# Column sums of the later modulation on TensorE: eight one-column products, or four products with 32 columns of ones and two transposes

## The chip, the cores and the metric

The kernel runs on one core of one Trainium2 chip. Its time is the device time of that core in microseconds (us). A core has TensorE (matrix products, PE in the profile; PEld is its weight load), VectorE (DVE), ScalarE (ACT), GpSimd (POOL) and SyncE (SP), which issues the transfers (DMA). Each engine works through its own instructions in a fixed order; semaphores make one wait for another. Products are written to PSUM, everything else lies in SBUF.

## What is computed

One layer of a streaming encoder, for 512 prompt frames and 64 sample frames, in float32. A condition vector c of each of the two streams gives six modulation vectors of 2048; two of them shift and scale the input, the others gate the residuals and shift and scale the input of the second part.

```python
mod = jax.nn.silu(c) @ w_ada[l] + b_ada[l]
sh1, sc1, g1, sh2, sc2, g2 = jnp.split(mod[:, None, :], N_MOD, axis=-1)
h = rmsnorm(x, norm1[l]) * (1 + sc1) + sh1
mix, s_a, s_b, s_c = token_mixers(h, ...)
x = x + g1 * mix
h = rmsnorm(x, norm2[l]) * (1 + sc2) + sh2
f, s_f = conv_ffn(h, ...)
x = x + g2 * f
y = rmsnorm(x, final_norm)
```

`token_mixers` is an input projection, two kinds of recurrence (GLA with 4 heads, gated DeltaNet with 8) and an output projection; `conv_ffn` is an up projection, a short convolution and a down projection. `w_ada` is 2048 x 12288 numbers, 100.7 MB.

## The kernel before

Feature vectors lie on the 128 partitions, frames along the free dimension. Every float32 weight tile is split into two parts, wh (ScalarE) and wl (VectorE, line 600), and each group of a projection is six products of 288 columns (lines 512 and 514).

The stages in order of time: a head, in which the modulation of the first two vectors and the normalised input are made (its `modulation` uses products with 32 output columns, four quarters of PSUM at a time, line 672); the input projection, 50 tiles of 16 groups each (`in_tile`), beside which the recurrences run as jobs; the first half of the output projection, 16 tiles of 8 groups; its second half, 16 tiles, which reads eight further inputs; the up projection; the down projection.

**The later modulation.** Vectors 2 to 5 are made beside the projections. They are 16 blocks of 512 columns of `w_ada` (`ada_blocks(range(8, 24))`). For a block, VectorE multiplies tiles of `w_ada` by the condition and adds them up in two accumulators acc (one for each stream, 128 x 512, lines 770 and 772), a partial sum on each partition; eight loads of 512 KB bring the tiles into the two buffers xr. Line 778 then adds up the 128 partitions: eight products, each with 128 columns of acc as the stationary operand and one column of ones as the moving one. `put_mod` (line 747) adds the bias and stores the result in mod. acc has a single buffer for each stream, so the next block's first multiplication (line 770) waits for the products.

**What sets the order.** `ada_block` is a Python generator: every `yield` is one step. `tick` is called after each projection group and moves it on by `ADA_RATE = 0.65` steps. `rest(n)` yields n times without work. A block has 32 steps with one VectorE operation each and `rest(4)` ahead of the products. Whatever is left of the generator when the first half of the output projection has been issued is then issued in one go (`for _ in K.ada: pass`). A scheduler afterwards places the instructions in each engine's queue.

**Around the end of the blocks.** In the first half of the output projection each tile m takes an xr buffer for the input (`x_tile`, lines 1093 and 1094, transposed on PE), and its result is added to the residual (line 1070, `residual`). The second half's inputs od0 to od7 are loaded by `load_o` (line 1077) into xr and into the three raw buffers in turn, and split by ScalarE (1079) and VectorE (1080). The raw buffers also take the weights (line 598).

Of the kernel before, what the change touches and what calls it, by code (L numbers as in the profile page):

```python
# [8 lines left out]
F32 = mybir.dt.float32  # L9
F32R = mybir.dt.float32r  # L10
I32 = mybir.dt.int32
AF = mybir.ActivationFunctionType
ALU = mybir.AluOpType
# [3 lines left out]
P = 128  # L17
D = 2048
KD = 16
# [76 lines left out]
class Kern:  # L96
# [483 lines left out]
    def raw(self):  # L580
        return self.wp.tile([P, 1024], F32, tag="raw", bufs=3, name=self.name("raw"))
# [161 lines left out]
            nc.sync.dma_start(self.halves(self.early[name, h]), acc[:, :, :HP])  # L743
            nc.sync.dma_start(self.halves(self.sd[name][:, h * TS:(h + 1) * TS]), acc[:, :, HP:])

    def put_mod(self, mi, k0, m):
        self.nc.vector.tensor_tensor(
            self.mod[:, mi, k0:k0 + 4], m,
            self.vec("b_ada", mi * KD + k0, 4).unsqueeze(2).to_broadcast([P, 4, 2]), op=ALU.add)

    def scale_mod(self, out, mi, norm, k0, n=4):

# [4 lines left out]
    def ada_block(self, blk, acc, raw):  # L757

        nc = self.nc
        V, T = nc.vector, nc.tensor  # L760
        acc = [a() for a in acc]
        for k0 in range(0, KD, 2):
            w = raw().rearrange("p (k n) -> p k n", k=2)
            nc.sync.dma_start(w, self.i["w_ada"][0, k0 * P:(k0 + 2) * P, blk * 512:(blk + 1) * 512]
                              .rearrange("(k p) n -> p k n", p=P))
            for k in range(2):
                for s in range(2):
                    col = self.ct[:, s, k0 + k:k0 + k + 1]
                    if k0 + k == 0:
                        V.tensor_scalar_mul(acc[s], w[:, k], col)  # L770
                    else:
                        V.scalar_tensor_tensor(acc[s], w[:, k], col, acc[s], op0=ALU.mult, op1=ALU.add)  # L772
                    yield
        yield from self.rest(4)
        pc = self.bank()
        for j in range(4):
            for s in range(2):
                T.matmul(pc[:, 2 * j + s:2 * j + s + 1], acc[s][:, j * P:(j + 1) * P], self.c["ones"][:, 0:1],  # L778
                         start=True, stop=True)
        self.put_mod(blk // 4, 4 * (blk % 4), pc[:, :8].rearrange("p (j s) -> p j s", s=2))  # L780

    def ada_blocks(self, blocks, acc):
        for blk in blocks:
# [901 lines left out]
```

## Time and profile before

| | |
|---|---|
| median of 3 runs | 2977.57 us (2977.28 to 2982.16) |
| the profiled execution's own time | 2988.47 us |
| its span, first to last instruction | 2986.8 us |
| mean granted TensorE clock | 0.978 |
| PE busy | 2871.2 us, 96% |
| VectorE busy | 2048.5 us, 69% |
| ScalarE busy | 1198.7 us, 40% |
| GpSimd busy | 334.5 us, 11% |
| transfers | 395.55 MB, mean 132 GB/s |
| line 772, multiplications of the blocks | 480 of 754 ns, 341.5 us of VectorE |
| line 778, products of the blocks | 128 products in 256 records |

The busy time of PE is that of its records, whose ends are modelled; how long a group of products holds PE is read from the start of the next. A row of the time line has start, length, engine, line, operation, output and inputs, and a count where rows are merged. The granted clock is 1.00 at full speed. The chain of waits is followed back from the last instruction.

### The profile page before, as it was taken

How to read it: one execution, taken by the hardware profiler on the slowest of the kernel's cores; microseconds unless marked ns; L12 is line 12 of the kernel's file. 1: busy time of each engine (PE TensorE's matmuls, PEld its weight loads, DVE VectorE, ACT ScalarE, POOL GpSimd, SP SyncE). 2: the span in 40 equal slices, each digit the busy share in tenths (PEclk: the TensorE clock that was granted, in tenths of full speed). 3: DMA queues.
4: the chain of work that ended last, by engine and by line, in shares of the span. 5: the costliest groups of instructions: out<-in, count | busy, mean ns of one | idle time of the engine just before them, and what ended most of it. 6: DMA issues, size and time to landing. Idle time of an engine off the chain costs nothing.

```text
span 2986.8 us, 52415 instructions
## 1 busy us (share of the span) xinstructions
PE 2871.2 (96%) x21096; PEld 2774.8 (93%) x21096; DVE 2048.5 (69%) x3198; ACT 1198.7 (40%) x2062; POOL 334.5 (11%) x609
## 2 busy tenths in 40 slices
PE   6998899999899999999999999999999999999998
PEld 3688889999799998999999999999999999999997
DVE  2355776667568867557888888888888865555555
ACT  4235454444435433245444444444444421222223
POOL 0004342232210000000011011111101100000000
PEclk7999999999899999999999999999999999999999
DMA  8964554445454446743333333333333473333221
GB/s 251 286 191 118 143 161 130 129 129 147 123 156 131 140 128 184 201 141 97 111 104 105 113 100 106 113 104 104 114 106 104 133 235 101 111 101 115 86 80 65
DMA packets 535446, 395.55 MB, mean 132 GB/s; under 512 B 59657, under 2 KB 465412, under 8 KB 535204
## 3 DMA queue, kind: packets, MB, share of 16 engines
q1 hardware_dynamic: 535204, 392.21, 44.7%
q8 instruction: 166, 2.72, 0.4%
q14 instruction: 76, 0.62, 0.1%
HBM read 356.47 MB, written 35.67 MB: 131 GB/s over the span
## 4 chain that ended last, share of the span: by engine, by line
PE 80%; DVE 6%; DMA 4%; POOL 4%; ACT 3%; issue 2%; SPq 0%; ACTq 0%; POOLq 0%; DVEq 0%
PE g L512 25%; PE g L514 13%; PE bank L1301 11%; PE bank L1300 11%; PE bank L1302 11%; DVE acc L772 2%; DMA xr<-in_w_ada_dram 1%; PE bank L144 1%; PE bank L672 1%; POOL m L352 1%; POOL m L351 1%; POOL s L138 1%; PE bank L405 1%; PE bank L778 1%; ACT m L1623 1%
## 5 line engine op out<-in xcount | busy, mean ns | idle before, releaser
L1301 PE MATMUL bank<-slot,wh 128*128 128x290 f32 x2464 | 736.2, 299 | 0.0
L1300 PE MATMUL bank<-slot,wh 128*128 128x290 f32 x2464 | 733.9, 298 | 0.0
L1302 PE MATMUL bank<-slot,wl 128*128 128x290 f32 x2464 | 728.0, 295 | 0.0
L512 PE MATMUL g<-slot,wh 128*128 128x288 f32 x3168 | 551.6, 295 | 0.2 <-DVE slot L1070 0.2
L512 PE MATMUL g<-hh,wh 128*128 128x288 f32 x2048 | 470.0, 308 | 2.4 <-ACT wh L599 2.4
L1302 PEld LDWEIGHTS bank<-slot,wl 128*128 128x128 f32 x2464 | 470.6, 191 | 0.0
L1301 PEld LDWEIGHTS bank<-slot,wh 128*128 128x128 f32 x2464 | 469.7, 191 | 0.1
L512 PEld LDWEIGHTS g<-slot,wh 128*128 128x128 f32 x3168 | 465.8, 188 | 0.7 <-DVE slot L1070 0.5
L1300 PEld LDWEIGHTS bank<-slot,wh 128*128 128x128 f32 x2464 | 464.1, 188 | 0.1
L514 PE MATMUL g<-hh,wl 128*128 128x288 f32 x2048 | 461.9, 304 | 1.2 <-DVE wl L600 1.2
L599 ACT ACTIVATE wh<-raw 128x1024 fp32r<-128x1024 f32 x215 | 227.2, 1058 | 586.6 <-PE g L512 571.4
L512 PE MATMUL g<-hl,wh 128*128 128x288 f32 x2048 | 460.6, 304 | 0.0
L1070 DVE SCALAR_TENSOR_TENSOR slot<-g,mod,slot 128x512 f32<-128x512 f32 (+1 forms) x448 | 201.9, 491 | 287.9 <-PE g L514 286.3
L772 DVE SCALAR_TENSOR_TENSOR acc<-xr,ct,acc 128x512 f32<-128x512 f32 x480 | 341.5, 754 | 29.0 <-DMA xr<-in_w_ada_dram 28.1
L512 PEld LDWEIGHTS g<-hh,wh 128*128 128x128 f32 x2048 | 337.7, 193 | 14.7 <-issue 10.2
L514 PEld LDWEIGHTS g<-hh,wl 128*128 128x128 f32 x2048 | 338.9, 193 | 8.3 <-issue 6.0
L514 PE MATMUL g<-slot,wl 128*128 128x288 f32 x1584 | 342.8, 295 | 0.0
L512 PEld LDWEIGHTS g<-hl,wh 128*128 128x128 f32 x2048 | 338.9, 193 | 4.1 <-issue 3.7
L600 DVE TENSOR_TENSOR wl<-raw,wh 128x1024 fp32r<-128x1024 f32 x215 | 262.0, 1219 | 64.9 <-ACT wh L599 63.3
L1247 ACT ACTIVATE wh<-raw 128x1024 fp32r<-128x1024 f32 x176 | 186.0, 1057 | 222.6 <-PE bank L1301 194.2
L514 PEld LDWEIGHTS g<-slot,wl 128*128 128x128 f32 x1584 | 255.3, 188 | 0.0
L1248 DVE TENSOR_TENSOR wl<-raw,wh 128x1024 fp32r<-128x1024 f32 x176 | 215.4, 1224 | 54.0 <-ACT wh L1247 54.0
(346 smaller groups left out, 3180.4 us busy)
## 6 DMA issues: line engine op xcount, KB each, us to landing
raw<-in_w_up_dram SPq DMA_DIRECT2D x176, 512.0 KB
xr<-in_w_ada_dram SPq DMA_DIRECT2D x128, 512.0 KB
raw<-in_w_in_dram SPq DMA_DIRECT2D x100, 512.0 KB
raw<-in_w_down_dram SPq DMA_DIRECT2D x88, 512.0 KB
hraw<-in_w_ada_dram SPq DMA_DIRECT2D x64, 512.0 KB
raw<-in_w_out_dram SPq DMA_DIRECT2D x32, 512.0 KB
slot<-actd SPq DMA_DIRECT2D x44, 288.0 KB
actd<-v SPq DMA_DIRECT2D x44, 256.0 KB
```

The costliest lines, as they stand in the source:

```text
L138: self.nc.gpsimd.tensor_tensor(out[:parts, :n], out[:parts, :n], self.mhalf[:parts, :n], op=ALU.pow)
L512: T.matmul(ps[:, h if bank is None else bank, :n], wh, x[:, h, :n], start=f, stop=False)
L514: T.matmul(ps[:, h if bank is None else bank, :n], wl, ah[:, h, :n], start=False, stop=stop)
L599: nc.scalar.activation(hi[:, :n_], raw[:, :n_], AF.Copy)
L600: nc.vector.tensor_tensor(lo[:, :n_], raw[:, :n_], hi[:, :n_].bitcast(F32), op=ALU.subtract)
L772: V.scalar_tensor_tensor(acc[s], w[:, k], col, acc[s], op0=ALU.mult, op1=ALU.add)
L1070: self.nc.vector.scalar_tensor_tensor(x1[:, :, z], ps[:, :, c], gain[:, q:q + 1], x1[:, :, z], op0=ALU.mult, op1=ALU.add)
L1247: self.nc.scalar.activation(hi, src, AF.Copy)
L1248: self.nc.vector.tensor_tensor(lo, src, hi.bitcast(F32), op=ALU.subtract)
L1300: T.matmul(ps, wh[:, j], hi, start=(c < 3 and j == 0), stop=False, skip_group_check=True)
L1301: T.matmul(ps, wh[:, j], lo, start=False, stop=False, skip_group_check=True)
L1302: T.matmul(ps, wl[:, j], hi, start=False, stop=(j == NPAIR - 1), skip_group_check=True)
```

## The change

In place of the eight products, four are made, with 32 columns of ones as the stationary operand and half of an accumulator (256 columns) as the moving one; each writes 32 partitions of one bank, so that partitions 0 to 31 hold the first half of the first stream's sums 32 times over, and so on. ScalarE copies the bank to SBUF (rows, in one of the three buffers qc of another tile), three steps without work follow, two transposes bring the sums back to the partitions, and `put_mod` is called twice with two tiles of 128 each.

```diff
-    def put_mod(self, mi, k0, m):
+    def put_mod(self, mi, k0, m, n=4):
         self.nc.vector.tensor_tensor(
-            self.mod[:, mi, k0:k0 + 4], m,
-            self.vec("b_ada", mi * KD + k0, 4).unsqueeze(2).to_broadcast([P, 4, 2]), op=ALU.add)
+            self.mod[:, mi, k0:k0 + n], m,
+            self.vec("b_ada", mi * KD + k0, n).unsqueeze(2).to_broadcast([P, n, 2]), op=ALU.add)
...
         yield from self.rest(4)
-        pc = self.bank()
-        for j in range(4):
-            for s in range(2):
-                T.matmul(pc[:, 2 * j + s:2 * j + s + 1], acc[s][:, j * P:(j + 1) * P], self.c["ones"][:, 0:1],
-                         start=True, stop=True)
-        self.put_mod(blk // 4, 4 * (blk % 4), pc[:, :8].rearrange("p (j s) -> p j s", s=2))
+
+        ps = self.bank()
+        for s in range(2):
+            for h in range(2):
+                r = 64 * s + 32 * h
+                T.matmul(ps[r:r + 32, :256], self.c["ones"][:, :32], acc[s][:, h * 256:(h + 1) * 256], start=True, stop=True)
+        rows = self.sp.tile([P, 256], F32, tag="qc", bufs=3, name=self.name("rows"))
+        self.nc.scalar.activation(rows, ps[:, :256], AF.Copy)
+        yield from self.rest(3)
+        pc = self.transpose4(rows.rearrange("p (b t) -> p b t", b=2), 2)
+
+        for h in range(2):
+            self.put_mod(blk // 4, 4 * (blk % 4) + 2 * h, pc.rearrange("p b (s c) -> p b s c", s=2)[:, :, :, 32 * h], 2)
```

With 39 steps instead of 36 a block, and one step's work in another place, the scheduler's order moves on all engines. Lines behind 778 have numbers higher by 7 after the change (1070 becomes 1077, 1077 becomes 1084, 1080 becomes 1087). Two places are shown. The first is PE's queue at the end of the blocks; before, the last block stands ahead of the twelfth tile's transposes in the first half (operands hh and hl):

```order
L512 MATMUL g_13022<-hl_12216,wh_13038 128x288 x2
L514 MATMUL g_13022<-hh_12215,wl_13039 128x288 x2
L778 MATMUL bank_13091<-consts_96,acc_12573 128x1
L778 MATMUL bank_13091<-consts_96,acc_12574 128x1
L778 MATMUL bank_13091<-consts_96,acc_12573 128x1
...
L144 MATMUL bank_13109<-consts_96,xr_13105 128x128 x4
L1099 MATMUL bank_13115<-consts_96,xr_13105 128x64
L512 MATMUL g_13103<-hh_12173,wh_13119 128x288 x2
```

After, on the same engine, it stands behind the last product of the sixteenth tile and ahead of the first of the second half (operands slot):

```order
L512 MATMUL g_13380<-hl_12179,wh_13396 128x288 x2
L514 MATMUL g_13380<-hh_12178,wl_13397 128x288 x2
L780 MATMUL bank_13478<-acc_13201,consts_96 32x256 x2
L780 MATMUL bank_13478<-acc_13202,consts_96 32x256 x2
L144 MATMUL bank_13485<-consts_96,rows_13483 128x128 x2
L512 MATMUL g_13562<-slot_13505,wh_13564 128x288 x2
L512 MATMUL g_13562<-slot_13506,wh_13564 128x288 x2
```

The last block's products have moved from the twelfth tile to the seam between the halves. The second place is VectorE's queue there. Before, behind the last multiplications stand the residuals of the later tiles with the splits of od between them:

```order
L772 SCALAR_TENSOR_TENSOR acc_12574<-xr_12990,ct,acc_12574 128x512
L1070 SCALAR_TENSOR_TENSOR slot_12944<-g_12943,mod,slot_12944 128x2x32
L600 TENSOR_TENSOR wl_13191<-raw_13189,wh_13190 128x1024
L1070 SCALAR_TENSOR_TENSOR slot_13023<-g_13022,mod,slot_13023 128x2x256
L747 TENSOR_TENSOR mod<-bank_13091,cols 128x8
L1070 SCALAR_TENSOR_TENSOR slot_13023<-g_13022,mod,slot_13023 128x2x32
L600 TENSOR_TENSOR wl_13262<-raw_13260,wh_13261 128x1024
L1080 TENSOR_TENSOR slot_13480<-raw_13477,slot_13479 128x576
```

After, from the sixteenth tile's residual on (eight of the ten multiplications left out; raw_13563 is the second half's first weight tile):

```order
L1077 SCALAR_TENSOR_TENSOR slot_13381<-g_13380,mod,slot_13381 128x2x256
L1077 SCALAR_TENSOR_TENSOR slot_13381<-g_13380,mod,slot_13381 128x2x32
L772 SCALAR_TENSOR_TENSOR acc_13201<-xr_13460,ct,acc_13201 128x512
...
L772 SCALAR_TENSOR_TENSOR acc_13202<-xr_13472,ct,acc_13202 128x512
L747 TENSOR_TENSOR mod<-bank_13485,cols 128x4 x2
L1087 TENSOR_TENSOR slot_13506<-xr_13503,slot_13505 128x576
L1087 TENSOR_TENSOR slot_13512<-raw_13509,slot_13511 128x576
L1087 TENSOR_TENSOR slot_13524<-raw_13521,slot_13523 128x576
```

All eight splits of od now stand behind the last block. SyncE's queue has the matching loads in that order too: the last four of `w_ada`, then od0 and od2, later od7, and then the second half's first weights:

```order
L764 DMA xr_13466<-in_w_ada_dram 128x2x512
L764 DMA xr_13472<-in_w_ada_dram 128x2x512
L1084 DMA xr_13503<-od_63 128x576
L1084 DMA xr_13515<-od_65 128x576
L1248 DMA raw_13554<-in_w_up_dram 128x8x128
L1084 DMA xr_13527<-od_67 128x576
L1084 DMA raw_13545<-od_70 128x576
L598 DMA raw_13563<-in_w_out_dram 128x8x128
```

What has moved is the tail of the last block: it stands ahead of the loads that the second half begins with.

## The prediction

> **What bounds the kernel now.** I read the page's busy shares and chain first, then busy time by stage, then the removed line and the last stretch in which it runs. Page:
>
> ```profile
> PE 2871.2 (96%) x21096; PEld 2774.8 (93%) x21096; DVE 2048.5 (69%) x3198; ACT 1198.7 (40%) x2062; POOL 334.5 (11%) x609
> ...
> PE 80%; DVE 6%; DMA 4%; POOL 4%; ACT 3%; issue 2%; SPq 0%; ACTq 0%; POOLq 0%; DVEq 0%
> ```
>
> TensorE (PE) is the bound: 96% busy and 80% of the chain. All sixteen later modulation blocks run between about 200 us and the end of the first half of the output projection. Busy time of that stretch and the next, clock, DMA share and GB/s behind:
>
> ```profile
> 200.00:1297.00 1097.00, 1031.90 (x7562) 989.37 (x7561) 746.31 (x1303) 488.83 (x1111) 211.12 (x433) 0.97 0.52 146
> 1297.00:1399.00 102.00, 102.00 (x775) 102.00 (x774) 70.59 (x127) 55.99 (x102) 4.81 (x17) 1.00 0.34 105
> ```
>
> Here PE stands idle for 65 us of 1097 (6%), and in the second half of the projection for none. What shortens PE's work in the first stretch is therefore worth about 94% of itself; what holds PE up at the end of it is paid in full.
>
> **The removed products.** The line's own view, with who waited for it, and the time line around one block (start, length, count):
>
> ```profile
> L778 PEld LDWEIGHTS bank<-consts,acc x256: 186/192/192, 286.0 to 1259.3; 128*128 128x128 f32 x128
> L778 PE MATMUL bank<-consts,acc x256: 164/250/271, 286.1 to 1259.3; 128*128 128x1 f32 x128
> ...
>   DVE acc L770: 20.6, 9
> ```
> ```profile
> 402.55 0.42 PE L514 MATMUL g<-hh,wl 128*128 128x288 f32 x2
> 402.81 1.84 PE L778 MATMUL bank<-consts,acc 128*128 128x1 f32 x16
> 404.52 0.51 PE L512 MATMUL g<-hh,wh 128*128 128x288 f32 x2
> ```
>
> A block's eight products are 16 records, one weight load each, and hold PE from 402.81 to 404.52: 1.71 us. Sixteen blocks: 27.4 us go.
>
> **The added products.** The same form with 32 output columns stands in the kernel's beginning (line 672, four quarters of PSUM, 512 moving columns), and transposes of four tiles too:
>
> ```profile
> 147.14 0.43 PE L514 MATMUL g<-hh,wl 128*128 128x288 f32 x2
> 147.50 1.07 PE L672 MATMUL bank<-hraw,cs 128*32 128x512 f32 x8
> 148.49 0.54 PE L512 MATMUL g<-hh,wh 128*128 128x288 f32 x2
> ...
> 169.62 0.43 PE L512 MATMUL g<-hl,wh 128*128 128x288 f32 x2
> 169.90 0.60 PE L144 MATMUL bank<-consts,rw 128*128 128x128 f32 x4
> 170.25 0.52 PE L514 MATMUL g<-hh,wl 128*128 128x288 f32 x2
> ```
> ```profile
> 143.06 1.05 PE L672 MATMUL bank<-hraw,cs 128*32 128x512 f32 x2
> ```
>
> One product alone (two records) takes 1.05 us, four take 1.07: they do run together. Two products before 147.50 end their slot at about 147.41, so four products hold PE for 1.08 us up to 148.49. With 256 columns instead of 512 it is between 0.54 (all of it scales) and 1.08 (none does). I take 0.70, nearer to half, because the columns halve and only the change of form stays. Four transposes hold PE from 169.90 to 170.25, so two cost 0.18 (0.35 at most). New price 0.88 us, saving 0.83 us a block, 13.3 us in all (4.5 to 15.8); at 94% **12.5 us**.
>
> Here a rule speaks against the change. The Trainium skill, "TensorEngine Tiling (Array Packing)", section "Key Properties", says that a change of tiling mode drains the engine. The 1.08 us above holds both changes of mode, so the rule can only mean that less of it scales. If none did, the products would cost 0.38 us more a block, 6 us in all, and the sum below would be 2984 us. No run here shows the 256-column form; the rows alone leave both ends open.
>
> **The clock behind the removed products.** Granted clock (third number from the end) behind four of the sixteen groups:
>
> ```profile
> 404.50:408.00 3.50, 3.50 (x28) 3.50 (x28) 3.50 (x8) 3.46 (x6) 0.14 (x1) 1.00 0.13 10
> 728.00:731.40 3.40, 3.40 (x16) 3.40 (x17) 2.18 (x5) 0.00 (x0) 0.00 (x0) 0.50 0.08 6
> 1205.50:1209.00 3.50, 3.50 (x18) 3.50 (x18) 1.92 (x4) 0.00 (x0) 0.00 (x0) 0.55 0.92 280
> 1260.30:1263.70 3.40, 3.40 (x15) 3.40 (x16) 0.80 (x1) 0.52 (x2) 0.00 (x0) 0.53 0.55 143
> ```
>
> After three of the sixteen the clock is at half for about 3.4 us although PE did not wait; the others look like the first row. One-column products evidently can count as rest. Dense 256-column products should not: 3 x 3.4 x 0.48 = **5 us** gained (0 to 5).
>
> **Off PE.** Added are sixteen ScalarE copies and sixteen more VectorE additions. Their nearest rows:
>
> ```profile
> L1052 ACT ACTIVATE m<-bank 128x256 f32<-128x256 f32 x16 | 5.4, 382 | 2.8 <-PE bank L144 2.5
> L747 DVE TENSOR_TENSOR mod<-bank,cols x16: 156/159/168, 289.3 to 1259.6; 128x8 f32<-128x8 f32 x16
> ```
>
> That is 16 x 0.38 = 6.1 us on ScalarE (45% busy in the stretch) and 16 x 0.16 = 2.5 us on VectorE (68%): hidden, 8.6 us at worst. The new wait is PE's transposes on the copy. Behind them all of PE queues, but in the printed order mostly 24 or more projection products (0.13 us each) stand between, over 3 us for a 0.38 us copy: free, except in the first block (six) and the last (none). Against it, VectorE's 20.6 us of waiting for line 778 mostly go, since the new block's first multiplication now comes three steps after the products; and with 39 steps a block instead of 36, fewer multiplications crowd the recurrence's work. Between nothing and 20.6 us; as PE was idle only 6% of the time I take **3 us**.
>
> **What the three extra steps do at the end.** The generator moves 0.65 steps per projection product group. Fifty input tiles of 16 groups and sixteen of 8 make 928 groups, 603 steps. Before, the blocks need 16 x 36 + 1 = 577: they end early. After, they need 16 x 39 + 1 = 625: 22 steps are left when the first half of the projection is over and are issued in one go, and the printed order keeps them there. Before, at this seam, VectorE's last multiplications and PE's first product of the second half:
>
> ```profile
> 1250.80 2.74 DVE L772 SCALAR_TENSOR_TENSOR acc<-xr,ct,acc 128x512 f32<-128x512 f32 x4
> ```
> ```profile
> 1297.18 0.70 PE L512 MATMUL g<-slot,wh 128*128 128x288 f32 x4
> ```
>
> The last multiplications were over 44 us before PE passed to the second half (operand slot instead of hh) without a gap. After, ten multiplications follow the last residual on VectorE, PE's four products stand right behind the last first-half product, and the splits of the second half's inputs and weights behind all of that. Prices:
>
> ```profile
> 1227.87 3.92 DMA xr<-in_w_ada_dram
> ...
> 542.44 5.54 DMA xr<-in_w_ada_dram
> ```
> ```profile
> 2898.59 3.59 DMA raw<-in_w_down_dram
> ...
> 1186.52 6.01 DMA raw<-in_w_out_dram
> ```
> ```profile
> 1297.38 0.94 DVE L1070 SCALAR_TENSOR_TENSOR slot<-g,mod,slot 128x512 f32<-128x512 f32 x2 [2.31 <-PE g L514]
> 1298.24 0.74 DVE L1080 TENSOR_TENSOR slot<-xr,slot 128x576 fp32r<-128x576 f32 x1
> ```
> ```profile
> L599 ACT ACTIVATE wh<-raw 128x1024 fp32r<-128x1024 f32 x215 | 227.2, 1058 | 586.6 <-PE g L512 571.4 <-DMA raw<-in_w_out_dram 10.2 <-PE bank L1301 4.5
> ```
>
> From the end of PE's last first-half product, in us: residual 0.9; two multiplications (2.74 / 4 each) to 2.3, which free the buffer for the last load of w_ada (two xr buffers); that load, between 3.9 and 5.5, say 4.9, to 7.2; its four multiplications to 9.9; products, copy and transposes 1.3, to 11.2; two additions to 11.5; three splits of 0.74, to 13.7, which free the raw buffer of the second half's first weights (SyncE's load waits for the third); that load (3.6 to 6.0), say 5, to 18.7; ScalarE's conversion 1.06, to 19.8. Only then does PE go on. The clock after a shorter pause:
>
> ```profile
> 1164.00:1167.00 3.00, 0.64 (x5) 0.41 (x3) 0.00 (x0) 1.02 (x2) 0.21 (x3) 1.00 0.88 271
> 1167.00:1171.80 4.80, 4.25 (x18) 4.02 (x19) 4.13 (x5) 2.84 (x6) 0.00 (x0) 0.64 0.57 170
> ```
>
> After about 2.4 us without work, 4.8 us ran at 0.64: 1.7 us lost; likewise here, 21.5. Less the 0.9 already charged to the last block: **+21 us**. At least 15 (ten multiplications without a wait, the shortest load, full clock); at most 26 (both longer loads, the clock lost twice).
>
> **Sum.** -12.5 - 5 - 3 + 21 = +0.5 us. The profiled execution (span 2986.8, time 2988.47) would take 2989.0. It lies 0.37% above the median of the runs, 2977.57; taken to the median the forecast is 2978 us, no change. About 0.2%, 6 us, is what a measurement can tell from none, so "within" is 2972 to 2984.
>
> **Rivals.**
> *Slower: the seam is not paid back.* The seam's rows are sure, since nothing stands beside it on PE, while the saving is spread over places where PE next waits for a recurrence anyway, and the clock may dip at other pauses. With 8 us from the products, 3 from the clock, none from VectorE and a seam of 22: +11, 2989 us. It decides once the blocks return under 15 us. For it: 65 us of idle PE beside the blocks. Against it: 94% busy. Chance 0.31.
> *Faster: the recurrence gains.* VectorE's 20.6 us wait stood ahead of work that PE awaits. If 10 us of it show, with 12.5 and 5, and the seam is 17 (loads near 4 us): -10.5, 2967 us. For it: DVE and DMA hold 10% of the chain. Against it: PE idles little. Chance 0.24.
> *The products do not run together.* Four times about 0.55, plus 0.18: 2.4 us a block, +11 instead of -12.5, in all about +24, 3002 us. The equal 1.05 and 1.07 us speak against it. Chance 0.04.
> *Forecast*, 0.41.
>
> **How the numbers follow.** Predicted 2978. The likeliest case's own range is 2972 to 2984. All low bounds together would give 2964 (-15.8 - 5 - 8 + 15), all high ones 2999 (-4.5 + 26); both at once are unlikely. To leave out about 2 in 10 I take 2966 to 2993, which holds the first two rivals' times. Slower 0.31 + 0.04 = 0.35, faster 0.24, same 0.41.
>
> **What would show it.** The new products with a slot near 0.7 us and the two transposes near 0.2; full clock behind every group; VectorE's wait on line 770 nearly gone; PE idle for some 18 us, in two pieces around the last block's products, between the two halves of the output projection; the second half itself unchanged at 102 us. Wrong would be: no gap there (the order would not bind), products above 1.1 us, or a stretch before the seam shortened by far more or less than 20 us.

## The result and the profile after

The changed kernel takes **2994.87 us** (median of 5 runs, 2993.45 to 2998.69) against 2977.57 us (median of 5, 2974.81 to 2984.28): ratio 1.0055, 95% interval 1.004 to 1.007, 17.3 us more. Its profiled execution took 2994.57 us (span 2992.8), so the two profiles lie only 6.0 us of span apart. The first profile of before was simply a long execution: over all runs here the kernel before took between 2968.7 and 2988.3 us, and the profiled one 2988.47. A second execution of it was therefore profiled (e1 below: 2973.54 us, span 2971.8); the second profile, with the first, brackets what is normal.

Busy times and shares of the chain, page of the changed kernel:

```profile
PE 2853.2 (95%) x21000; PEld 2747.7 (92%) x21000; DVE 2047.4 (68%) x3214; ACT 1198.2 (40%) x2076; POOL 340.9 (11%) x609
...
PE 78%; DVE 5%; POOL 5%; DMA 5%; issue 3%; ACT 3%; SPq 1%; ACTq 0%; POOLq 0%; DVEq 0%
```

TensorE is still the bound, busy for 18 us less and with a smaller share of the chain. For the comparison by stage I cut each trace at three instructions that all kernels have (lines in the changed kernel's numbers): ScalarE's first instruction of line 927, just ahead of the blocks; its last copy into an operand slot (line 1107), near the end of the first half of the output projection; and its first instruction of line 1136, in the second half. Windows of before (first profile), of before (second profile) and of after: length, then busy time of PE, PEld, DVE, ACT, POOL, the granted clock, DMA share and GB/s.

```profile
199.40:1291.30 1091.90, 1026.80 (x7524) 984.27 (x7523) 744.27 (x1303) 487.93 (x1108) 211.49 (x435) 0.97 0.52 146
```
```profile
195.30:1277.30 1082.00, 1019.41 (x7525) 976.17 (x7524) 743.88 (x1303) 487.36 (x1109) 216.92 (x435) 0.97 0.52 148
1277.30:1297.70 20.40, 20.40 (x156) 20.40 (x156) 9.44 (x15) 7.58 (x14) 0.19 (x1) 1.00 0.42 123
```
```profile
196.90:1276.00 1079.10, 1007.90 (x7417) 955.64 (x7416) 726.10 (x1294) 483.07 (x1114) 216.95 (x435) 0.97 0.49 141
1276.00:1320.10 44.10, 26.98 (x184) 24.84 (x183) 25.58 (x39) 13.07 (x22) 0.18 (x1) 0.77 0.78 219
1320.10:1407.60 87.50, 87.45 (x662) 87.25 (x662) 65.05 (x117) 50.50 (x96) 5.56 (x16) 1.00 0.34 109
```

The seam grew from 20.4 (20.7 in the first profile) to 44.1 us, with PE busy for 27 of them; the second half itself is as before. The stretch with the blocks became 12.8 us shorter than in the first profile, but only 2.9 us shorter than in the second. It can be split further: the marks of idle time on PE's rows add up to its waits, the granted clock in windows of 1 us adds up to the time lost to it, and PE's busy time less that loss is its work at full clock.

| stretch with the blocks, us | before, first | before, second | after |
|---|---|---|---|
| length | 1091.9 | 1082.0 | 1079.1 |
| PE's work at full clock | 989.3 | 990.4 | 978.9 |
| lost to the clock | 37.5 | 29.0 | 29.0 |
| PE's waits | 64.6 | 62.0 | **70.3** |

Against the second profile the work fell by 11.5 us and the waits rose by 8.3; the clock gave nothing. With 1.6 us ahead of the stretch, 23.7 at the seam and -1.4 behind it, that is the 21.0 us between these two spans.

The new products, view of their line in after (instructions with least, median and greatest duration in ns; below, who waited for them):

```profile
L780 PE MATMUL bank<-acc,consts x128: 379/403/634, 283.1 to 1291.7; 128*32 128x256 f32 x128
...
  ACT rows L782: 40.2, 14
  DVE acc L770: 8.1, 5
```

VectorE's wait for the products (20.6 us before) is mostly gone, as foretold. One block's products on after's time line:

```profile
554.63 0.43 PE L512 MATMUL g<-hl,wh 128*128 128x288 f32 x2
554.90 0.43 PE L514 MATMUL g<-hh,wl 128*128 128x288 f32 x2
555.25 0.64 PE L780 MATMUL bank<-acc,consts 128*32 128x256 f32 x8
555.82 0.53 PE L512 MATMUL g<-hh,wh 128*128 128x288 f32 x2
556.19 0.43 PE L512 MATMUL g<-hl,wh 128*128 128x288 f32 x2
```
```profile
632.55 0.38 PE L144 MATMUL bank<-consts,rows 128*128 128x128 f32 x2
632.68 0.52 PE L512 MATMUL g<-hh,wh 128*128 128x288 f32 x2
633.03 0.43 PE L512 MATMUL g<-hl,wh 128*128 128x288 f32 x2
```

The slot is 0.57 us for the products and 0.13 for the transposes. The neighbours lose a little too: two projection records usually take 0.27 us from start to start, here 0.35 ahead of the products and 0.37 behind them. With that a block costs 0.75 + 0.21 = 0.96 us; the old one, counted alike, 1.79 (slot 1.71, then 0.35). That is 0.83 us a block, the saving that was foretold, though by other terms (below).

PE at the seam, and the clock there:

```profile
1281.84 0.42 PE L514 MATMUL g<-hh,wl 128*128 128x288 f32 x2
1290.65 1.64 PE L780 MATMUL bank<-acc,consts 128*32 128x256 f32 x8 [8.38 <-DVE acc L772]
1292.77 0.69 PE L144 MATMUL bank<-consts,rows 128*128 128x128 f32 x2 [0.48 <-ACT rows L782]
1301.71 1.33 PE L512 MATMUL g<-slot,wh 128*128 128x288 f32 x4 [8.25 <-ACT wh L599]
```
```profile
1293.40:1301.70 8.30, 0.06 (x1) 0.00 (x0) 5.09 (x10) 4.59 (x7) 0.00 (x0) 0.50 0.97 277
1301.70:1306.80 5.10, 5.09 (x25) 4.81 (x26) 3.18 (x3) 1.74 (x2) 0.00 (x0) 0.66 1.10 300
```

From the last first-half product (ends at 1282.26) to the first of the second half: 19.5 us, in two pieces around the last block's products, and 5.1 x 0.34 = 1.7 us of clock behind.

Where most of the waits rose: PE's transposes at the start of a recurrence, in before (first profile; 33.1 us of idle time in the second) and after (group; busy, mean ns; idle before it and what ended it):

```profile
L144 PE MATMUL bank<-consts,m 128*128 128x128 f32 x158 | 31.6, 303 | 34.4 <-ACT m L1623 33.4 <-DVE m L1623 1.0
```
```profile
L144 PE MATMUL bank<-consts,m 128*128 128x128 f32 x158 | 32.0, 309 | 42.9 <-ACT m L1630 40.0 <-DVE m L1630 2.4
```

One of these waits in after, and the same place in the second profile of before:

```profile
532.25 0.69 DVE L362 TENSOR_TENSOR m<-cm,consts 128x512 f32<-128x512 f32 x1 [6.56 <-DMA cm<-d]
532.86 0.16 DVE L137 TENSOR_SCALAR s<-s 128x4 f32<-128x4 f32 x1
...
533.10 1.38 POOL L138 TENSOR_TENSOR s<-s,mhalf 128x4 f32<-128x4 f32 x1 [5.46 <-DVE s L137]
534.52 1.28 ACT L1630 ACTIVATE m<-m,s 128x128 f32<-128x128 f32 x4 [8.42 <-POOL s L138]
534.97 0.48 PE L144 MATMUL bank<-consts,m 128*128 128x128 f32 x1 [7.82 <-ACT m L1630]
```
```profile
521.80 0.17 DVE L137 TENSOR_SCALAR s<-s 128x4 f32<-128x4 f32 x1 [0.95 <-ACT sq L1630]
522.06 1.01 POOL L138 TENSOR_TENSOR s<-s,mhalf 128x4 f32<-128x4 f32 x1 [0.38 <-DVE s L137]
523.10 1.28 ACT L1630 ACTIVATE m<-m,s 128x128 f32<-128x128 f32 x4 [1.33 <-POOL s L138]
523.55 0.33 PE L144 MATMUL bank<-consts,m 128*128 128x128 f32 x1 [0.90 <-ACT m L1630]
...
525.24 0.69 DVE L362 TENSOR_TENSOR m<-cm,consts 128x512 f32<-128x512 f32 x1 [3.27 <-DMA cm<-d]
```

A small addition on VectorE (line 137) starts the chain VectorE, GpSimd, ScalarE, PE. Before, it stands ahead of line 362, which waits for a transfer of the next recurrence. In the changed kernel's queue line 362 stands first, VectorE stands at the transfer for 6.56 us, and PE for 7.82. So it is at three starts (waits of 7.82, 5.26 and 4.61 us, near 535, 612 and 687 us), and at none in before, where in turn one start near 760 loses 10 us while VectorE stands at a load of `w_ada`.

### The profile page after: what moved, and what is told of

The parts are those of the page before. It is cut to its first block, busy times and chain, and to the rows that moved or that the text cites. A ratio compares the mean times of both kernels' runs of the same rounds, so it can differ in the third digit from the quotient of the medians.

```text
span 2992.8 us, 52262 instructions
## 1 busy us (share of the span) xinstructions
PE 2853.2 (95%) x21000; PEld 2747.7 (92%) x21000; DVE 2047.4 (68%) x3214; ACT 1198.2 (40%) x2076; POOL 340.9 (11%) x609
## 4 chain that ended last, share of the span: by engine, by line
PE 78%; DVE 5%; POOL 5%; DMA 5%; issue 3%; ACT 3%; SPq 1%; ACTq 0%; POOLq 0%; DVEq 0%
PE g L512 25%; PE g L514 13%; PE bank L1308 11%; PE bank L1307 11%; PE bank L1309 11%; DVE acc L772 2%; PE bank L144 2%; POOL m L352 2%; POOL m L351 1%; PE bank L672 1%; DMA xr<-in_w_ada_dram 1%; PE bank L405 1%; POOL s L138 1%; ACT m L1630 1%; DVE m L1630 1%
```

## The experiments

"Old" means the eight one-column products, "new" the four products with copy and transposes. Time: median, with its ratio to the kernel before on the same chip (medians 2977.6 to 2981.0) and 95% interval. Runs of different chips are best compared by the ratios. Stretch, waits, clock and seam are those of the run's one profile, as defined above. Some expectations quote 68.6, 59.7 and 48.5 us of waits for e4, e6 and e5; with each wait counted once they are 68.0, 58.7 and 49.0, and no reading changes by it.

| run | products, steps, rate | time | ratio | stretch | waits | clock | seam |
|---|---|---|---|---|---|---|---|
| after | new, 39, 0.65 | 2994.9 | 1.0055 (1.004 to 1.007) | 1079.1 | 70.3 | 29.0 | 44.1 |
| e1 | old, 36, 0.65 (before again) | 2973.5, one execution | | 1082.0 | 62.0 | 29.0 | 20.4 |
| e2 | old, 39, 0.65 | 3019.2 | 1.0130 (1.0113 to 1.0147) | 1099.8 | 70.4 | 42.6 | 45.0 |
| e3 | new, 39, 0.70 | 2974.8 | 0.9991 (0.9977 to 1.0004) | 1078.5 | 69.3 | 32.4 | 19.8 |
| e4 | new, 36, 0.65 | 2970.2 | 0.9975 (0.9965 to 0.9986) | 1075.9 | 68.0 | 29.0 | 20.3 |
| e5 | old, 36, 0.70 | 2967.3 | 0.9975 (0.9961 to 0.9988) | 1079.8 | 49.0 | 37.5 | 19.7 |
| e6 | new, 36, 0.70 | 2959.1 | 0.9937 (0.9923 to 0.9950) | 1063.9 | 58.7 | 25.6 | 20.1 |
| e7 | old, 36, 0.63 | 2966.6 | 0.9960 (0.9948 to 0.9973) | 1069.3 | 53.9 | 18.7 | 21.0 |
| e8 | new, 36, 0.63 | 2969.8 | 0.9971 (0.9959 to 0.9984) | 1078.2 | 66.7 | 29.0 | 23.3 |
| e9 | new, 36, 0.65, late copy | 2973.2 | 0.9977 (0.9966 to 0.9988) | 1078.5 | 68.5 | 30.7 | 20.0 |
| e10 | a quarter of old, 36, 0.65 | 2959.6 | 0.9930 (0.9917 to 0.9943) | 1070.7 | 69.7 | 32.4 | 19.9 |
| e11 | as e9, 0.70 | 2959.6 | 0.9929 (0.9916 to 0.9943) | 1066.3 | 59.7 | 25.6 | 19.9 |
| e12 | after, narrow multiplications | 2984.6, one execution | | 1072.1 | 58.4 | 27.3 | 38.5 |
| e13 | after, addition on GpSimd | 2991.1 | 1.0036 (1.0023 to 1.0049) | 1073.7 | 66.3 | 29.0 | 43.2 |
| e14 | before, addition on GpSimd | 2976.5 | 0.9986 (0.9976 to 0.9996) | 1083.3 | 64.7 | 25.6 | 19.8 |
| e15 | e4, addition on GpSimd | 2974.3 | 0.9989 (0.9980 to 0.9998) | 1081.9 | 71.9 | 32.4 | 20.1 |
| e16 | e6, addition on GpSimd | 2954.8 | 0.9911 (0.9897 to 0.9924) | 1060.1 | 56.3 | 22.2 | 20.0 |
| e17 | e4, products three times | 2980.2 | 1.0001 (0.9992 to 1.0010) | 1086.8 | 64.5 | 23.9 | 20.2 |
| e18 | e6, products three times | 2981.3 | 1.0001 (0.9990 to 1.0011) | 1083.7 | 59.6 | 25.6 | 19.9 |

### The seam: e1 to e4

**e1**, the kernel before profiled again.

> The kernel before, unchanged but for empty lines, profiled a second time, since its first profiled execution took 2988.47 us where the median of its runs is 2977.57. Theory A (the blocks return only some 4 us): the stretch up to the last product of the first half is shorter in this execution by about 11 us than the 1297.1 us of the first profile, so that the 14.7 us by which the changed kernel came to that place earlier were mostly the first profile's own delay. Rival B (the blocks return some 15 us and something behind the first half takes 11 back): that place is again at 1295 to 1299 us, and the time lies near 2988 or what is behind it is shorter.

The end of the first half came at 1277.3 us instead of 1291.3 (the 1297.1 us of the expectation is the place where PE passed on), 14.0 us earlier, of which 4.1 were gained ahead of the blocks. Theory A: against this execution the changed kernel is at that place only 1.3 us earlier.

**e2**, the three steps alone, with the old products.

```diff
-        yield from self.rest(4)
+        yield from self.rest(7)
```

> The kernel before with its 16 one-column products, but 7 empty steps ahead of them instead of 4, so that a block takes 39 steps as in the changed kernel. If the three steps and the seam they make cost 21 us: 2977.6 + 21 = 2999 us, PE idle for 18 us around the last block. If the seam is partly hidden and the rest of the change's loss lies in the products: under 2987 us.

The seam is there, with the old products:

```profile
1314.68 3.72 PE L778 MATMUL bank<-consts,acc 128*128 128x1 f32 x16 [10.78 <-DVE acc L772]
1327.02 1.33 PE L512 MATMUL g<-slot,wh 128*128 128x288 f32 x4 [8.63 <-ACT wh L599]
```

It costs 24.6 us (45.0 against 20.4), but the time rose by 41 us, not 21: the stretch ahead of it is 17.8 us longer than in e1, by 8.4 us of waits and 13.6 us of clock, while the work in it fell by 4.3 us, in part because the last block moved out. So the steps cost something besides the seam, which no term had. The three starts of a recurrence at which PE waits in the changed kernel wait here too, 9.0, 8.2 and 5.4 us near 544, 622 and 699 us, and VectorE stands 7.7, 7.2 and 4.6 us at a transfer right ahead of line 137: that order does not need the new products. Against this twin the new products gain 24 us.

**e3**, the pace raised so that 39 steps fit, and **e4**, 36 steps with the new products.

```diff
-JOB_RATE, ADA_RATE = 1.0, 0.65
+JOB_RATE, ADA_RATE = 1.0, 0.70
```

> The changed kernel with the generator moved by 0.70 steps a group instead of 0.65: 0.70 x 928 = 650 steps for the 625 needed, so the last block is done some 127 matmul rows ahead of the second half, as before the change. If the seam is the whole loss: 2994.9 - 21 = 2974 us, under the kernel before by the 4 us that the blocks return by the medians. If the blocks return 15 us as the two profiles have it: 2963 us. Rival (the recurrences, met by other multiplications, lose the time): 2985 us or more, with the gap at the seam gone.

```diff
-        yield from self.rest(4)
+        yield from self.rest(1)
```

> The changed kernel with one empty step ahead of the products instead of 4, and three ahead of the transposes as it has: 36 steps a block as in the kernel before, transposes at the place of the old products. If the three steps are the whole loss: 2974 us as with the higher rate; the products now come one step after the last multiplications, and if PE waits there for VectorE, up to 1 us a block more, 2990 us.

Both came as the seam theory has it: 2974.8 and 2970.2 us, 20 and 25 us under the changed kernel. The seam's window in e3 holds no idle time:

```profile
1276.60:1296.40 19.80, 19.80 (x152) 19.80 (x151) 9.17 (x15) 7.62 (x14) 0.18 (x1) 1.00 0.42 125
```

The waits ahead of it stayed at 69 and 68 us. At 0.65 either half of the change lifts them by itself: with the old products they are 62 to 65 us for 36 steps and 70.4 for 39, with the new ones 68.0 and 70.3. The seam is thus shown to be the larger part of the loss; what is left is why 36 steps with the new products gain 8 us, and not 12.5 or more.

### Pace, and twins with old and new products: e5 to e8

> The kernel before (16 one-column products, 36 steps a block), its generator moved by 0.70 steps a group instead of 0.65, nothing else. Theory C (PE's waiting in the recurrences is a matter of where the multiplications happen to fall, and the kernel before falls well): PE waits 68 to 72 us in the stretch up to the last first-half product instead of 62 to 65, and its clock loses some more at the one-column groups; 2982 to 2990 us. Rival D (the waits come with the new products, by the transposes and the copy): 61 to 65 us of waiting, 2974 to 2980 us.

> The new products with one empty step ahead of them (36 steps a block) at 0.70 steps a group: the twin of the old products at 0.70. Theory C: the waits are those of its twin within 3 us, and the time is 12 to 20 us under it (12.5 from the products, 0 to 8 from the clock behind the one-column groups). Rival D: 7 us more waiting than the twin, the time at most 8 us under it.

> The kernel before at 0.63 steps a group: blocks 3% further apart, the last one done 39 matmul rows (some 5 us) ahead of the second half. Theory C: 66 to 72 us of waiting up to the last first-half product, and 2980 to 2995 us. Rival D: 61 to 65 us and 2974 to 2982 us.

> The new products with one empty step ahead of them (36 steps a block) at 0.63 steps a group, the twin of the old products at 0.63. Theory C: waits as in the twin within 3 us, the time 12 to 20 us under it. Rival D: 7 us more waiting than the twin, the time at most 8 us under it.

Theory C fell at once: the old products at 0.70 and 0.63 wait less than in the kernel before (49.0 and 53.9 us) and are faster by 10 and 11 us (by the ratios 7 and 12). The pace alone, with nothing else changed, thus moves the time by some 10 us. D's numbers for these two runs fell as well. Of the twins, the new ones have 13.4 us less work both times, but 9.7 and 12.8 us more waits; to the clock they lose 12 us less at 0.70 and 10 us more at 0.63. They are 8 us faster at 0.70 and 3 us slower at 0.63. These differences between the twins are near D's numbers; its cause (copy and transposes) is not shown.

### What the waits hang on: e9 to e12

**e9** and **e11**, the copy two steps later (at 0.65 and 0.70; the edit is against e4 and e6).

```diff
+        yield from self.rest(2)
         self.nc.scalar.activation(rows, ps[:, :256], AF.Copy)
-        yield from self.rest(3)
+        yield from self.rest(1)
```

> The new products in 36 steps a block at 0.65 (one empty step ahead of them), with the ScalarE copy two steps later, so that it is issued when the products are mostly done, and the transposes one step behind it. Theory S (ScalarE comes to the copy too early, stands 19.1 us in all waiting for the products, and the recurrence's copies behind it are late): ScalarE's wait there falls under 5 us, PE's waits up to the end of the first half from 68.6 to 58 to 62 us, 2970 falls to about 2961 us. Rival P (with shorter products PE only comes earlier to places where a recurrence's own chain over ScalarE and VectorE ends last): PE's waits stay at 66 to 71 us, 2966 to 2974 us.

> The late copy at 0.70 steps a group, the twin of the 2959 us kernel with new products at 0.70, whose PE waits 59.7 us and whose ScalarE waits 14.6 us at the copy. Theory S: PE's waits about 50 us as with the old products at 0.70 (48.5), 2949 to 2953 us. Rival P: 58 to 62 us, 2956 to 2962 us.

Nothing moved in time or waits. But the wait that was to go did not go either (the copy's own view in e9):

```profile
its engine sat idle before it (us, times) until:
  PE bank L780: 18.5, 11
```

ScalarE still stood 18.5 us at the copy (19.1 in e4). The runs show that moving the copy by two steps of the generator doesn't matter here, and leave theory S undecided.

**e10**, a quarter of the old products (the modulation's other columns are left out, as the expectation says).

```diff
-        for j in range(4):
+        for j in range(1):
...
-        self.put_mod(blk // 4, 4 * (blk % 4), pc[:, :8].rearrange("p (j s) -> p j s", s=2))
+        self.put_mod(blk // 4, 4 * (blk % 4), pc[:, :2].unsqueeze(1).to_broadcast([P, 4, 2]))
```

> The kernel before with 2 of its 8 one-column products a block (the other three quarters of the modulation's columns are left out, and the sums of the first quarter are put in their place): 20.5 us less work on TensorE, with no copy, no transposes, the same steps and the same place. Rival P: PE's waits rise from 62 to 65 us to 72 us or more, and only 8 to 12 of the 20.5 us come out: 2966 to 2970 us. Theory S: the waits stay as they are, and the time falls by 20 to 25 us, to 2953 to 2958 us.

By the medians the time fell by 21 us, so all of the work came out, as S has it. The profiled execution, the longest of the six (2965.5 us), has 69.7 us of waits and is 8 us shorter than e1, nearly as P has it. Undecided, though it shows that waits can rise to 70 us without copy or transposes.

**e12**, narrow multiplications (most columns of the sums are left out; one execution).

```diff
-                        V.scalar_tensor_tensor(acc[s], w[:, k], col, acc[s], op0=ALU.mult, op1=ALU.add)
+                        V.scalar_tensor_tensor(acc[s][:, :64], w[:, k, :64], col, acc[s][:, :64], op0=ALU.mult, op1=ALU.add)
```

> The changed kernel with VectorE's multiplications from the second row of weights on done for 64 of the 512 columns only (the other columns of the sums are left out); loads, steps and products stay. It asks what PE's transposes at the start of a recurrence wait for (40.0 us on ScalarE's m in the changed kernel). Theory V (VectorE's queue, filled by these multiplications, is late there): under 25 us, all of PE's waits under 55 us instead of 70.3. Rival P (the recurrence's own chain): 36 to 42 us, all 65 us or more. By either the seam gets shorter by about 6 us, the nine multiplications in it.

```profile
L144 PE MATMUL bank<-consts,m 128*128 128x128 f32 x158 | 32.1, 305 | 36.6 <-ACT m L1630 35.7 <-DVE m L1630 0.7
```

Theory V fell: 35.7 us on ScalarE's m, against 40.0 in the changed kernel. The length of VectorE's multiplications is not what the transposes mainly wait for. All waits were 58.4 us, between the two theories; the seam shrank by 5.6 us (44.1 to 38.5), as foretold.

### VectorE standing at a transfer: e13 to e16

The addition of line 137 goes to GpSimd, which has the next step anyway.

```diff
-        self.nc.vector.tensor_scalar_add(out[:parts, :n], src[:parts, :n], EPS)
+        self.nc.gpsimd.tensor_tensor(out[:parts, :n], src[:parts, :n], self.eps[:parts, :n], op=ALU.add)
...
+        K.eps = K.cp.tile([P, 8], F32, name="eps")
+        nc.vector.memset(K.eps, EPS)
```

> The changed kernel, with the addition ahead of each inverse root (one small VectorE operation) done by GpSimd, which computes the root anyway; nothing else. Theory Q (PE's waits at the starts of the recurrences come from VectorE, which by its order stands waiting for a transfer, of the recurrence's inverse or of w_ada, right ahead of that small addition): the waits of PE's transposes on ScalarE's m between 400 and 800 us fall from 23.1 to under 10 us, and with the clock behind them the time from 2995 to 2970 to 2980 us. Rival G (GpSimd's own queue takes VectorE's place, or the chain's own length decides): 18 us or more of waits, 2990 us or more.

> The kernel before with the same addition on GpSimd. Theory Q: its 14.5 to 15.1 us of such waits, most of it one wait of 10 us near 760, fall to under 8 us, and the time from 2978 to 2963 to 2970 us. Rival G: no change.

> The new products in 36 steps a block at 0.65, with the same addition on GpSimd: the twin of the kernel before with it. Theory Q: waits as in the twin within 4 us (without it 19.6 against 14.5), so that the products' work of 12.5 us comes out, 12 to 20 us under the twin, near 2950 us. Rival P (shorter products only lengthen waits): 4 to 8 us under the twin.

> The new products in 36 steps a block at 0.70, with the same addition on GpSimd. Theory Q: waits between 400 and 800 us from 23.4 to under 10 us, the time from 2959 to 2936 to 2946 us. Rival G: no change, 2955 to 2962 us.

The named waits went as Q says: between 400 and 800 us from 23.1 to 8.6 in e13, 14.5 to 8.0 in e14, 19.6 to 6.0 in e15, 23.4 to 12.1 in e16 (there not quite under the 10 of the forecast). At the place shown above, VectorE in e13 still stands at the transfer, and PE no longer stands with it:

```profile
536.60 1.28 ACT L1632 ACTIVATE m<-m,s 128x128 f32<-128x128 f32 x4 [2.82 <-POOL s L138]
537.05 0.43 PE L144 MATMUL bank<-consts,m 128*128 128x128 f32 x1 [2.35 <-ACT m L1632]
...
539.89 1.29 DVE L362 TENSOR_TENSOR m<-cm,consts 128x512 f32<-128x512 f32 x2 [6.53 <-DMA cm<-d]
```

But the times fell by some 4 us at most (by the ratios 4 to 8), far from Q's figures, and e15 is no faster than e4. PE's waits in all are 66.3, 64.7, 71.9 and 56.3 us against 70.3, 62.0 to 64.6, 68.0 and 58.7: others took their place, in e13 above all at line 244:

```profile
L244 PE MATMUL bank<-m,m 128*128 128x64 f32 x144 | 20.9, 294 | 13.7 <-DVE m L1632 9.4 <-ACT m L1632 2.7 <-DVE mod L747 1.6
```

(7.5 us in after.) So it is shown that at these starts PE waited because VectorE stood at a transfer; that the stretch as a whole loses by it is not shown: without it, most of the time is lost at other places.

### TensorE's work put back: e17 and e18

```diff
-        for s in range(2):
+        for s in (0, 1, 0, 1, 0, 1):
             for h in range(2):
                 r = 64 * s + 32 * h
```

> The new products in 36 steps a block at 0.65, but each block's four products made three times over into the same bank: some 1.1 us a block, 17 us in all, of TensorE's work put back at their place, with no VectorE or ScalarE work. Rival P (what the shorter products save between the recurrences mostly turns into waiting for them): PE's waits fall from 68.6 to 60 to 64 us and the time rises from 2970 only to 2974 to 2979 us. Linear (work on TensorE counts in full): waits stay, 2985 to 2989 us.

> The same at 0.70 steps a group. Rival P: waits from 59.7 to 52 to 55 us, the time from 2959 to 2963 to 2968 us. Linear: 2974 to 2978 us.

At 0.65, 19.3 us of work cost 10 us (2970.2 to 2980.2; 8 by the ratios): waits -3.5, clock -5.1. That is just outside P's figures and further from the linear ones, and more of it came from the clock than from the waits. At 0.70, 18.9 us of work cost 22 us (19 by the ratios), with the same clock and 0.9 us more waits. P is roughly borne out at one pace and not at the other.

## Why the prediction was wrong

**The products: right in sum, partly by luck.** 0.83 us a block was taken, 0.83 measured; the twins' work differs by 13.4 us, 13.3 were foretold. The terms came out otherwise. Counted as in the prediction, from where two projection products would have ended, the four products hold PE for 0.65 us (0.70 taken) and the transposes for 0.13 (0.18). That is 0.10 us less; but the projection products behind them lose 0.18 us more a block, 0.08 behind the old products, and this stood in no term. The prediction read the 1.08 us of its 512-column rows as holding both changes of form; they hold the delay ahead (0.09 us), not the one behind (0.10).

On the rule of drains (the Trainium skill, "TensorEngine Tiling (Array Packing)", section "Key Properties"): from 512 to 256 columns the 1.08 us became 0.65, so about 0.22 us of it did not scale, and 0.10 us behind it comes on top. A fixed cost of that size agrees with the rule, though no run tells a drain from other fixed costs; that nothing scales, 0.38 us a block more, does not agree with the trace.

That 94% of the work comes out was not borne out as a rule: put back, 19 us of work cost 8 to 10 us at 0.65 and 19 to 22 us at 0.70 (e17, e18).

**The clock: right in kind, mis-sized.** Behind the new products the clock never dipped unless PE also waited there, in none of twelve kernels with them (after, e3, e4, e6, e8, e9, e11, e13 and e15 to e18). The old ones lost 5.1 us in the first profile, 0 in the second, 8.5 in e2 and in e5, 1.7 in e7 and 0 in e14, with no wait of PE over 0.9 us just ahead. The same kind of group with and without it, the block at 717 us in e1 and the second block of e2:

```profile
719.00:722.40 3.40, 3.40 (x29) 3.40 (x30) 3.21 (x7) 0.01 (x1) 0.00 (x0) 1.00 0.01 2
```
```profile
357.60:361.00 3.40, 3.40 (x16) 3.40 (x17) 2.37 (x6) 1.76 (x5) 0.00 (x0) 0.50 0.00 0
```

The term of 5 us was a property of one execution, and of one that was 11 us over the median. Carrying the sum over to the median by the ratio of 0.37% kept a gain that the median had mostly made already.

**Off PE: the step that failed.** "Fewer multiplications crowd the recurrence's work ... I take 3 us" was a gain. Measured were 6 to 8 us of loss: PE's waits went from 62.0 to 64.6 up to 70.3 us. VectorE's wait for the products did go (20.6 to 8.1 us), but PE's waits did not fall with it. What moved is the order in VectorE's queue: at three starts of a recurrence it now stands at a transfer ahead of the addition that starts it, as it does in e2 with the old products in 39 steps. The prediction read the order at the two places it spoke of and costed the rest of the reordering at nothing. The copy was costed at its 0.38 us, while ScalarE stands 40.2 us at it, 16.1 of them at the seam; e9 could not take that away, so its share is open.

**The seam: right.** +21 was foretold, 15 to 26 as bounds; the window grew by 23.4 to 23.7 us, of which 0.9 was charged to the last block. By its steps: products 9.9 us after the last first-half product (8.4 measured), PE going on after 19.8 (19.5), clock 1.7 (1.7).

**The sum.** -12.5 - 5 - 3 + 21 was foretold. Against the first profile the stretch gave -12.8 (work -10.4, clock -8.5, waits +5.7, and 0.4 of rounding), and all in all +6.0 us, where +0.5 was foretold. Against the second it gave -2.9, and +21.0. The medians' 17.3 us lie between. Of the 20.5 us by which the second comparison misses the forecast, 11 are the waits off PE, 5 the clock, 3 the seam and 1 the products. The rival "the seam is not paid back" named the way and the threshold (the blocks return under 15 us); its 2989 us still held 8 us from the products net and 3 from the clock.

**What stays open:** why the recurrences' waits are 49 to 72 us depending on pace and products. The variants show that they move with each reordering, and that none of the single things that were changed makes them: not the copy's step, not the length of VectorE's multiplications, not the addition's engine. Shorter products are followed by longer waits at all three paces, but of work put back half is swallowed at 0.65, and none at 0.70.

**A faster kernel than both:** the new products with one empty step ahead of them at 0.70 steps a group (e6), 2959.1 us, and with the addition on GpSimd (e16), 2954.8 us, 0.89% under the kernel before (0.76 to 1.03%).

## What to carry to other kernels

When an edit adds steps to work that is woven into something else at a fixed rate, multiply out where that work now ends: three empty steps a block cost more than the faster products gained, and one number (the rate) took it back. Count a saving of the bounding engine only after asking what it meets next, compare the order of the helper engines at every place where they wait for a transfer, and put a twin at another pace beside the result, since pace alone moved this kernel by some 10 us. Profile the kernel before twice: a term taken from dips or waits of one execution may be that execution's own.

## What the runs showed of the hardware

A wait of PE can cost clock besides. Near waits, and behind the one-column products, the clock was at half for 3.4, 6.8, 10.2 or 13.7 us, so what was lost came in steps of 1.7 us: 1.7, 3.4, 5.1 or 6.8. The Trainium skill, "TensorE: Matmul & The Clock Gate", section "Part 1: The HAM clock gate (the "warmup" mystery)", has half or full clock decided over windows of 3.4 us; steps of half a window agree with that. Its section "HAM oscillation — how this bites in real kernels" warns of gaps over 3.4 us. Here shorter ones did it too. In the changed kernel's stretch with the blocks the clock was at half within 4 us behind all eight waits over 3.4 us, two of the three between 1.5 and 3.4 us, and none of the thirty from 0.15 to 1.5 us. Two short ones near each other were not free elsewhere, PE's only two waits between 560 and 577 us in e1, and the window:

```profile
560.67 1.09 PE L144 MATMUL bank<-consts,qkv 128*128 128x128 f32 x8 [1.17 <-ACT qkv L931]
568.87 1.08 PE L244 MATMUL bank<-m,m 128*128 128x64 f32 x8 [1.16 <-DVE m L1630]
```
```profile
560.00:577.00 17.00, 15.18 (x103) 14.10 (x104) 6.49 (x14) 6.36 (x28) 4.13 (x4) 0.80 0.34 96
```

These two waits of 1.2 us were followed by 17 x 0.20 = 3.4 us lost; what share the small products among them had is not shown. Behind 16 one-column records, with no wait of PE in the 10 us before, up to 5.1 us were lost (e5, half clock from 572.0 to 582.2 us).

The kernel before spread over 2968.7 to 2988.5 us in all its runs, the changed one over 5.2 us in its five. That the one-column products make the spread is not shown: e3, with the new products, spread over 18 us in twelve runs (2964.6 to 2982.8).
